# A transformer block on one core: W_out streamed over three and four raw places with low halves on VectorE alone, and the first sums of the second MLP product in other PSUM banks

## The chip, the cores and the metric

The kernel runs on one core of a Trainium2 chip. Its time is the device time of one execution in microseconds (us); 1531.92 us is the median of three runs. A profile is one execution recorded by the hardware profiler: PE is TensorE's matmuls, PEld its weight loads, DVE is VectorE, ACT is ScalarE, POOL is GpSimd, SP is the engine that issues most transfers.

## The reference

One block over x of 1024 tokens and 1024 features, all in float32:

```
u = rms_norm(x) * norm_mix_pre;   projections of u @ w_in
o_a = gated sparse attention;     o_b = sliding-window attention with sinks
y = sigmoid(gate_a) * (o_a @ w_up_nsa) + sigmoid(gate_b) * (o_b @ w_up_swa)
h = x + rms_norm(y @ w_out) * norm_mix_post
u = rms_norm(h) * norm_mlp_pre
f = square(relu(u @ w_mlp_in)) @ w_mlp_out
out = h + rms_norm(f) * norm_mlp_post
```

The change touches y @ w_out, and the first sums of the product with w_mlp_out.

## The kernel before, in words

Products run at nearly full float32 precision: each operand is split into a high half (a copy rounded to the matmul's input type, `wh`) and a low half (the operand less its high half, `wl`), and a product is three matmuls, high by high, high by low and low by high (`mm3`, lines 123 to 126). `split` (line 84) makes both halves: ScalarE copies, VectorE or GpSimd subtracts. `load_w` (line 96) loads a stretch of a weight into a tile called `wraw`, from a pool and with a number of places that the caller gives, and splits it. With no engine named it lets ScalarE make the high half (line 108) and deals out the subtraction (lines 115 and 116): five eighths to VectorE and three eighths to GpSimd. With an engine named it calls `split`, whose instructions have lines 87 and 91.

After attention the kernel computes y, transposed, in two halves of 512 tokens (`yh`, `yl`), line 773 on. At dc = 5 it already loads the first two rows of blocks of W_out into the pool `wo` (`wo_load`, two places) and splits the first.

`out_proj(c, ts_, nhs, xs_, at)`, line 837, is one pass of y @ W_out: two blocks of 128 tokens by all 1024 features, in four PSUM banks. It runs over eight steps k2. A step is one row of blocks of W_out, [128, 1024], 512 KB: a transfer, a split, and 12 matmuls (two token blocks, two halves of the features, three each). Four passes follow one another, c = 0 with blocks 0, 1 and then 2, 3, and c = 1 likewise, and each streams W_out anew. In pass 1 (`started` is empty) steps 0 and 1 use what `wo` holds, and steps 2 to 7 load into two places of the pool `wp2`, their halves into two places of `wp2`. From pass 2 on all eight steps load into the same two raw places, and the halves go into three places (`WEB`) of the pool `we`, which is opened after pass 1, when `wo` is closed. The low halves of c = 0 are dealt out to VectorE and GpSimd, those of c = 1 go to VectorE.

At the end of a pass ScalarE takes the sum of squares of each bank (line 874) and VectorE multiplies the bank by the gain (line 875). Then, for each block, come `norm_a` (residual h and its sum of squares, lines 884 to 894, with a store of h issued by GpSimd), `norm_b` (the second norm, line 899) and `norm_t` (eight transposes on TensorE, line 909, in two PSUM banks of their own with the tag `pt`, and splits of them). `load_x` loads rows of x; at step `at` of passes 1 and 2 ScalarE's queue issues it, held behind the last high half by `tc.issue_after(last_act[0].ins)` (line 851). `rstd_of` (line 139) has small instructions on both engines.

Behind the passes stand four `head`s of the MLP's first product (line 1004), then a loop over 16 blocks `mlp1` (line 1059), which makes a product of 2 x 2 blocks with seven products instead of eight, from sums and differences of its operands (`factor`, line 923, and lines 1065 and 1092). Their sums stand in PSUM tiles with the tag `ps`, six banks used in turn. The second product (`product`, line 1205) also has seven parts; the first, fifth, sixth and seventh add up in four banks `xs`, the others in four banks `ys`. Before, `xs` is allocated first, then `ys`.

The instructions of each engine stand in one order, fixed when the program is built: a list scheduler walks through the program with an estimate of how long things take, and gives each engine the first of its instructions, in program order, that is ready by that estimate. On the chip each engine then goes through its own list and waits where it must. Tiles with the same tag share places; a new one waits until the last reader of the old one is done.

Of the kernel before, what the change touches and what calls it, by code (L numbers as in the profile page):

```python
# [8 lines left out]
F32 = mybir.dt.float32  # L9
F32R = mybir.dt.float32r  # L10
AF = mybir.ActivationFunctionType
ALU = mybir.AluOpType
# [3 lines left out]
P = 128  # L16
T = 1024
D = 1024
NB = T // P
# [9 lines left out]
CUT = (5, 5)  # L29
# [5 lines left out]
WEB = 3  # L35
# [17 lines left out]
def tile_hybrid_block(ctx: ExitStack, tc: tile.TileContext, x, norm_mix_pre, norm_mix_post, norm_mlp_pre,  # L53
                      norm_mlp_post, w_in, cmp_pos_k, cmp_w1_k, cmp_w2_k, cmp_pos_v, cmp_w1_v, cmp_w2_v,
                      attn_sinks, rel_bias, w_up_nsa, w_up_swa, w_out, w_mlp_in, w_mlp_out, onehot, out):
    nc = tc.nc
# [3 lines left out]
    def pool(name, bufs=1, side="left", space=None):  # L60
        kw = {} if space is None else {"space": space}
        if space is not DRAM:
            kw["reuse_waits"] = "tile"
        if space is None:
            kw["side"] = side
        return tc.tile_pool(name=name, bufs=bufs, **kw)
# [17 lines left out]
    def split(h, l, src, h_eng="act", l_eng="dve"):  # L84

        if h_eng == "act":
            nc.scalar.activation(h, src, AF.Copy)  # L87
        else:
            nc.vector.tensor_copy(h, src)
        eng = nc.vector if l_eng == "dve" else nc.gpsimd  # L90
        eng.tensor_tensor(l, src, h.bitcast(F32), op=ALU.subtract)  # L91

    nw = [0]
    last_act = [None]

    def load_w(parts, shape, wpool=None, hb=2, l_eng=None, rpool=None, rb=2, cut=5, tag="w"):

        raw = (rpool or wp).tile([P] + shape, F32, name="wraw", tag="wraw", bufs=rb)
        for sl, ap in parts:
            nc.sync.dma_start(raw[sl] if sl is not None else raw, ap)  # L100
        wpool = wpool or wp
        h = wpool.tile([P] + shape, F32R, name="wh", tag=tag + "h", bufs=hb)
        l = wpool.tile([P] + shape, F32R, name="wl", tag=tag + "l", bufs=hb)
        nw[0] += 1
        if l_eng:
            split(h, l, raw, l_eng=l_eng)
        else:
            last_act[0] = nc.scalar.activation(h, raw, AF.Copy)
            if len(shape) == 1:
                hv, lv, rv = (t.rearrange("p (a b) -> p a b", a=8) for t in (h, l, raw))  # L110
            elif shape[0] < 8:
                hv, lv, rv = (t.rearrange("p k (a b) -> p (k a) b", a=8 // shape[0]) for t in (h, l, raw))
            else:
                hv, lv, rv = h, l, raw
            for eng, a, b in ((nc.vector, 0, cut), (nc.gpsimd, cut, 8)):
                eng.tensor_tensor(lv[:, a:b], rv[:, a:b], hv[:, a:b].bitcast(F32), op=ALU.subtract)
        return h, l
# [5 lines left out]
    def mm3(ps, ah, al, bh, bl, first, last):  # L123
        nc.tensor.matmul(ps, ah, bh, start=first, stop=False)  # L124
        nc.tensor.matmul(ps, ah, bl, start=False, stop=False)  # L125
        nc.tensor.matmul(ps, al, bh, start=False, stop=last)  # L126
# [27 lines left out]
    def transpose_split(ps_pool, tag, u, th, tl, b0, bufs):  # L154

        for k0 in range(0, NB, 4):
            pt = ps_pool.tile([P, 4, P], F32, name="pt", tag=tag, bufs=bufs)
            for j in range(4):
                nc.tensor.transpose(pt[:, j, :], u[:, (k0 + j) * P:(k0 + j + 1) * P], ident)
            split(th[:, k0:k0 + 4, b0:b0 + P], tl[:, k0:k0 + 4, b0:b0 + P], pt)  # L160
# [9 lines left out]
    with ExitStack() as s_u:  # L170
# [36 lines left out]
        with ExitStack() as s:  # L207
# [16 lines left out]
            def v_weights():  # L224
                for k in range(0, NB, 2):
                    raw = wp.tile([P, 2, NV], F32, name="vraw", tag="wraw", bufs=2)
                    for a, b, c in ((0, 128, C_VS), (128, 280, C_VW), (280, 408, C_VB)):
                        nc.sync.dma_start(raw[:, :, a:b], wr[:, k:k + 2, c:c + b - a])
                    split(vh[:, k:k + 2, :], vl[:, k:k + 2, :], raw)
# [180 lines left out]
        with ExitStack() as s:  # L410
# [328 lines left out]
            op = s_ot.enter_context(pool("ot"))  # L739
# [12 lines left out]
    with ExitStack() as s:  # L752
# [6 lines left out]
        wo = s_wo.enter_context(pool("wo", side="right"))  # L759
# [11 lines left out]
        with s_ot:  # L771
            dp = s_ot.enter_context(pool("dtmp"))
            for dc in range(8):
# [11 lines left out]
                for c in range(2):  # L785
                    ts = slice(c * 512, (c + 1) * 512)
                    t = []
# [26 lines left out]
        wp2 = s_w2.enter_context(pool("wq"))  # L814
# [12 lines left out]
        ep = s_e.enter_context(pool("etmp"))  # L827
# [1 line left out]
        eh = s_e.enter_context(pool("etmph"))  # L829
        hb_e.update({b: eh.tile([P, D], F32, name="hb", tag="hb", bufs=2) for b in (0, 1)})  # L830
        s_we = s_e.enter_context(ExitStack())
        ssp = [ep.tile([P, 2], F32, name="ssp", tag="ssp", bufs=8) for _ in range(NB)]

        hbs = {}
        started, we = [], []

        def out_proj(c, ts_, nhs, xs_=(), at=0):
            pss = {(t, nh): ps_any() for t in ts_ for nh in nhs}
            n = 1024 // (512 * len(nhs))
            for k2 in range(NB // n):  # L840
                if started or k2 > 1:
                    wh, wl = load_w([(None, wor[:, n * k2:n * k2 + n, 512 * nhs[0]:512 * nhs[-1] + 512])],
                                    [n, 512 * len(nhs)], *((we[0], WEB) if started else (wp2, 2)), cut=CUT[c],
                                    rpool=wp2, l_eng="dve" if c else None)
                elif k2:
                    wh, wl = (wp2.tile([P, 1, 1024], F32R, name=n_, tag="w" + n_[1], bufs=2) for n_ in ("wh", "wl"))
                    split(wh, wl, wo_raw[1])
                else:
                    wh, wl = wo_hl
                if k2 == at:  # L850
                    with tc.issue_after(last_act[0].ins):
                        for b in xs_:
                            load_x(b, nc.scalar)
                for j in range(n):
                    k = n * k2 + j
                    for t in ts_:
                        ts = slice(t * P, (t + 1) * P)
                        for i, nh in enumerate(nhs):
                            ns = slice(i * 512, (i + 1) * 512)
                            mm3(pss[t, nh], yh[c][:, k, ts], yl[c][:, k, ts], wh[:, j, ns], wl[:, j, ns],  # L860
                                k == 0, k == NB - 1)
            if not started:
                s_wo.close()
                we.append(s_we.enter_context(pool("we")))
            started.append(1)
            for t in ts_:
                b = c * 4 + t
                if b not in o1:
                    o1[b] = (ea if b % 4 < 2 else ep).tile([P, D], F32, name="o1",
                                                           tag="o1a" if b % 4 < 2 else "o1b", bufs=2)  # L870
                for nh in nhs:
                    ns = slice(nh * 512, (nh + 1) * 512)
                    junk = we[0].tile([P, 512], F32, name="junk", tag="junk", bufs=1)
                    nc.scalar.activation(junk, pss[t, nh], AF.Square, accum_out=ssp[b][:, nh:nh + 1])
                    nc.vector.tensor_tensor(o1[b][:, ns], pss[t, nh], gpost[:, ns], op=ALU.mult)
# [4 lines left out]
        def load_x(b, eng=None):  # L880
            hbs[b] = hb_e[b] if b in hb_e else (eh if b < 4 else ea).tile([P, D], F32, name="hb", tag="hb", bufs=2)
            (eng or nc.sync).dma_start(hbs[b], x[b * P:(b + 1) * P, :])
# [40 lines left out]
        def factor(i, b):  # L923
# [17 lines left out]
            split(bh[i][:, :, hs], bl[i][:, :, hs], src)  # L941

        out_proj(0, (0, 1), (0, 1), (0, 1), 4)
        norm_a(0)
        norm_a(1)
        norm_b(0)
        norm_b(1)
        load_x(2)
        load_x(3)
        out_proj(0, (2, 3), (0, 1), (4, 5), 3)  # L950
        norm_t(0)
        norm_t(1)
        norm_a(2)
        norm_a(3)
        norm_b(2)
        norm_b(3)
        out_proj(1, (0, 1), (0, 1))
        norm_t(2)
        norm_t(3)
# [193 lines left out]
            return p.tile([P, 2, 512], F32R, name=name, tag=name, bufs=n)  # L1153

        pq = s.enter_context(pool("ps3", space=PSUM))
        xs = [pq.tile([P, 512], F32, name=f"xs{t}") for t in range(4)]
        ys = [pq.tile([P, 512], F32, name=f"ys{t}") for t in range(4)]
        w2v = w_mlp_out.rearrange("(q e p) (j c) -> e j p q c", e=2, p=P, j=2)
        NK = NPAIR // 2
        b2 = {}  # L1160
# [170 lines left out]
```

## Time and profile before

| what | value |
|---|---|
| median of three runs | 1531.92 us (1530.36 to 1532.13) |
| the profiled execution, its own time | 1533.06 us |
| its span (first to last instruction) | 1531.3 us |
| mean granted TensorE clock | 0.989 of full |
| TensorE busy | 1472.2 us (96%) |
| VectorE, ScalarE, GpSimd busy | 1042.8, 792.9, 343.1 us |
| the four passes of y @ W_out | about 763.6 to 874.1 us of the span |
| the second product begins | 1215.35 us |

How to read it: a line of the profile names the line of the kernel, the engine, the operation, the tile written and the tiles read. A line can be that of a helper. "Idle before <- X" is the time for which the engine had nothing to do and the instruction that ended it. The chain is followed back from the last instruction, at each step to what released it.

### The profile page before, as it was taken

Reading aid. Unit: us, or ns where it says so; the run is one execution under the profiler, and the core shown is the slowest. Engines: PE = TensorE matmul, PEld = TensorE weight load, DVE = VectorE, ACT = ScalarE, POOL = GpSimd, SP = SyncE. Lnnn points to the kernel's source line nnn. Section 1 sums busy time; section 2 is a strip of 40 time slices with the busy share of each in tenths; the row PEclk is TensorE's granted clock in tenths of the full one; section 3 lists DMA queues with packets and bytes.
Section 4 is the critical chain, followed back from the end, with each engine's and each line's share of the span. In section 5 each row is a group of like instructions: output and inputs, shape, how many; then the busy total and the mean of one; then the engine's idle time right before and its main releaser. Section 6 shows DMA issues by size and latency. Waiting matters only on the chain.

```text
span 1531.3 us, 19921 instructions
## 1 busy us (share of the span) xinstructions
PE 1472.2 (96%) x6924; PEld 1205.1 (79%) x6924; DVE 1042.8 (68%) x2094; ACT 792.9 (52%) x1529; POOL 343.1 (22%) x281
## 2 busy tenths in 40 slices
PE   8998999999999999999989968999999999999997
PEld 6997888778887788888866756888888788888886
DVE  7454774588855988737547789866666655594775
ACT  5343775598854988664346663333322334334533
POOL 2000451100001000031042015775655300000302
PEclk9999999999999999999999988999999999999999
DMA  8723125111132111174256662453443696353551
GB/s 241 236 88 83 39 53 158 42 39 38 39 97 58 44 35 42 32 271 165 82 201 240 209 175 83 159 176 126 162 150 122 235 376 241 110 192 98 172 172 55
DMA packets 161335, 204.27 MB, mean 133 GB/s; under 512 B 14801, under 2 KB 104945, under 8 KB 161234
## 3 DMA queue, kind: packets, MB, share of 16 engines
q1 hardware_dynamic: 152880, 178.05, 36.8%
q0 software_dynamic: 7344, 21.53, 4.1%
q10 hardware_dynamic: 1010, 3.41, 0.6%
q8 instruction: 54, 0.88, 0.2%
q14 instruction: 47, 0.39, 0.1%
HBM read 152.50 MB, written 58.32 MB: 138 GB/s over the span
## 4 chain that ended last, share of the span: by engine, by line
PE 81%; DVE 7%; DMA 6%; ACT 3%; issue 2%; POOL 1%; SPq 0%; DVEq 0%; ACTq 0%; POOLq 0%
PE xs L1224 10%; PE ys L1224 9%; PE mm L124 7%; PE mm L125 7%; PE mm L126 7%; PE ps L1000 6%; PE ps L998 6%; PE ps L999 6%; PE pt L532 5%; DMA wraw<-in_w_out_dram 4%; PE o L545 2%; PE o L544 2%; PE s L499 2%; PE s L500 2%; PE ps L126 2%
## 5 line engine op out<-in xcount | busy, mean ns | idle before, releaser
L124 PE MATMUL mm<-uh,wh 128*128 128x512 f32 x464 | 200.0, 431 | 4.1 <-DVE qb L458 3.2
L126 PE MATMUL mm<-uh,wl 128*128 128x512 f32 x464 | 183.9, 397 | 0.0
L125 PE MATMUL mm<-ul,wh 128*128 128x512 f32 x464 | 183.7, 396 | 0.0
L91 DVE TENSOR_TENSOR tl<-pt,th 128x512 fp32r<-128x512 f32 x162 | 110.5, 686 | 42.3 <-ACT th L87 41.4
L512 ACT ACTIVATE e<-e,nm 128x256 f32<-128x256 f32 (+7 forms) x192 | 124.2, 649 | 19.9 <-DVE nm L506 19.5
L87 ACT ACTIVATE wh<-wraw 128x1024 fp32r<-128x1024 f32 x71 | 75.2, 1058 | 109.4 <-PE mm L125 36.7
L91 POOL TENSOR_TENSOR wl<-wraw,wh 128x1024 fp32r<-128x1024 f32 x16 | 38.4, 2402 | 413.0 <-ACT wh L87 381.1
L87 ACT ACTIVATE th<-pt 128x512 fp32r<-128x512 f32 (+1 forms) x178 | 104.2, 591 | 51.0 <-PE pt L532 43.3
L87 ACT ACTIVATE fh<-fraw 128x1024 fp32r<-128x1024 f32 x56 | 59.5, 1062 | 135.9 <-PE xs L1224 70.0
L91 DVE TENSOR_TENSOR fl<-fraw,fh 128x1024 fp32r<-128x1024 f32 x56 | 69.5, 1242 | 74.8 <-ACT fh L87 74.4
L126 PEld LDWEIGHTS mm<-uh,wl 128*128 128x128 f32 x464 | 87.4, 188 | 20.5
L1224 PE MATMUL xs<-vh,fh 128*128 128x512 f32 x256 | 100.3, 392 | 2.3 <-ACT c L1109 2.3
L91 DVE TENSOR_TENSOR wl<-wraw,wh 128x1024 fp32r<-128x1024 f32 x55 | 69.3, 1260 | 47.9 <-ACT wh L87 47.6
L532 PE MATMUL pt<-ident,e 128*128 128x128 f32 x648 | 101.1, 272 | 0.3 <-DVE tl L91 0.2
L124 PEld LDWEIGHTS mm<-uh,wh 128*128 128x128 f32 x464 | 88.0, 190 | 16.8 <-issue 3.3
L1224 PE MATMUL xs<-vl,fh 128*128 128x512 f32 x256 | 100.3, 392 | 0.0
L1224 PE MATMUL xs<-vh,fl 128*128 128x512 f32 x256 | 100.1, 391 | 0.0
L125 PEld LDWEIGHTS mm<-ul,wh 128*128 128x128 f32 x464 | 88.3, 190 | 11.8
L532 PEld LDWEIGHTS pt<-ident,e 128*128 128x128 f32 x648 | 80.7, 140 | 18.4 <-issue 0.5
L87 ACT ACTIVATE ws_h<-wraw 128x512 fp32r<-128x512 f32 x48 | 30.3, 631 | 118.8 <-PE ps L999 117.9
L1247 POOL TENSOR_TENSOR cc<-cc,gB 128x512 f32<-128x512 f32 x14 | 24.4, 1765 | 269.0 <-ACT sq L1246 267.3
L998 PE MATMUL ps<-bh,ws_h 128*128 128x512 f32 x192 | 77.7, 406 | 5.3 <-ACT ws_h L87 4.2
(298 smaller groups left out, 4011.4 us busy)
## 6 DMA issues: line engine op xcount, KB each, us to landing
fraw<-f_d SPq DMA_DIRECT2D x48, 512.0 KB, 3.6
wraw<-in_w_mlp_in_dram SPq DMA_DIRECT2D x36, 512.0 KB, 4.6
wraw<-in_w_out_dram SPq DMA_DIRECT2D x32, 512.0 KB, 3.5
f_d<-q SPq DMA_DIRECT2D x64, 256.0 KB, 3.8
b<-in_w_mlp_out_dram SPq DMA_DIRECT2D x32, 512.0 KB, 10.8
wraw<-in_w_in_dram SPq DMA_DIRECT2D x27, 512.0 KB, 4.7
f_d<-c SPq DMA_DIRECT2D x44, 256.0 KB, 4.3
gate_d<-gst SPq DMA_DIRECT2D x32, 256.0 KB, 2.0
```

The source lines that it names most:

```text
L87: nc.scalar.activation(h, src, AF.Copy)
L91: eng.tensor_tensor(l, src, h.bitcast(F32), op=ALU.subtract)
L124: nc.tensor.matmul(ps, ah, bh, start=first, stop=False)
L125: nc.tensor.matmul(ps, ah, bl, start=False, stop=False)
L126: nc.tensor.matmul(ps, al, bh, start=False, stop=last)
L499: nc.tensor.matmul(ps[:, :w], qs[r][:, qcol], kh, start=True, stop=False)
L512: nc.scalar.activation(e[:, :n], e[:, :n], AF.Exp, scale=-1.0, bias=nm[:, r:r + 1], accum_out=sm[:, r:r + 1])
L532: tr = nc.tensor.transpose(pt[:rows, r, :], es[r][:, off:off + rows], ident)
L998: nc.tensor.matmul(ps, ah[:, k, :], bh[i][:, k, :], start=n[0], stop=False, skip_group_check=True)
L999: nc.tensor.matmul(ps, ah[:, k, :], bl[i][:, k, :], start=False, stop=False, skip_group_check=True)
L1000: nc.tensor.matmul(ps, al[:, k, :], bh[i][:, k, :], start=False, stop=n[1], skip_group_check=True)
L1224: nc.tensor.matmul(bank[t], l_[:, j, ts], r_[:, j, :], start=a_, stop=z_, skip_group_check=True)
```

## The change

`out_proj` gets its raw places from other pools: steps 4 and 5 of pass 1 from `wo` (beside two of `wp2` for steps 2, 3, 6 and 7), and steps 2 and 5 of the later passes from a new place in `we` (beside two of `wp2`). All low halves of W_out go to VectorE, as `split` makes them, and `split` notes its high half in `last_act`. The sums of squares of eight blocks stand in two tiles instead of eight. In the second product `ys` is allocated first, and `xs` behind it, with its tiles 2 and 3 ahead of 0 and 1.

```diff
     def split(h, l, src, h_eng="act", l_eng="dve"):
         if h_eng == "act":
-            nc.scalar.activation(h, src, AF.Copy)
+            last_act[0] = nc.scalar.activation(h, src, AF.Copy)
...
-        eng.tensor_tensor(l, src, h.bitcast(F32), op=ALU.subtract)
+        return eng.tensor_tensor(l, src, h.bitcast(F32), op=ALU.subtract)
...
-        ssp = [ep.tile([P, 2], F32, name="ssp", tag="ssp", bufs=8) for _ in range(NB)]
+        ssps = [ep.tile([P, 4, 2], F32, name="ssp", tag="ssp", bufs=2) for _ in range(2)]
+        ssp = [ssps[b // 4][:, b % 4] for b in range(NB)]
...
                     wh, wl = load_w([(None, wor[:, n * k2:n * k2 + n, 512 * nhs[0]:512 * nhs[-1] + 512])],
-                                    [n, 512 * len(nhs)], *((we[0], WEB) if started else (wp2, 2)), cut=CUT[c],
-                                    rpool=wp2, l_eng="dve" if c else None)
+                                    [n, 512 * len(nhs)], *((we[0], WEB) if started else (wp2, 2)), l_eng="dve",
+                                    **(dict(rpool=we[0], rb=1) if started and k2 % 3 == 2 else
+                                       dict(rpool=wo) if not started and k2 % 4 < 2 else dict(rpool=wp2)))
...
-        xs = [pq.tile([P, 512], F32, name=f"xs{t}") for t in range(4)]
         ys = [pq.tile([P, 512], F32, name=f"ys{t}") for t in range(4)]
+        xs = [pq.tile([P, 512], F32, name=f"xs{t}") for t in (2, 3, 0, 1)]
+        xs = xs[2:] + xs[:2]
```

## Rows read from the trace of the kernel before

**Rows 1.** The profile's page: busy time of the engines; chain of waits by line.

```profile
PE 1472.2 (96%) x6924; PEld 1205.1 (79%) x6924; DVE 1042.8 (68%) x2094; ACT 792.9 (52%) x1529; POOL 343.1 (22%) x281
...
PE xs L1224 10%; PE ys L1224 9%; PE mm L124 7%; PE mm L125 7%; PE mm L126 7%; PE ps L1000 6%; PE ps L998 6%; PE ps L999 6%; PE pt L532 5%; DMA wraw<-in_w_out_dram 4%; PE o L545 2%; PE o L544 2%; PE s L499 2%; PE s L500 2%; PE ps L126 2%
```

**Rows 2.** The chain of waits, by line, from 760 to 880 us.

```profile
by line: DMA wraw<-in_w_out_dram 48.0%; POOL wl L116 9.7%; DVE wl L91 8.2%; ACT wh L87 7.9%; issue 6.8%; ACT wh L108 5.3%; DMA wraw<-in_w_mlp_in_dram 3.7%; ACT junk L874 2.3%; PE ps L1000 1.6%; PE ps L999 1.1%; PE ps L998 1.1%; ACT L143 1.1
```

**Rows 3.** Passes 1 to 4: us, busy PE to POOL, clock, DMA share, GB/s.

```profile
763.60:790.60 27.00, 23.41 (x98) 17.58 (x96) 8.35 (x10) 8.54 (x9) 9.83 (x6) 1.00 0.60 204
790.60:821.80 31.20, 26.80 (x112) 19.10 (x112) 21.38 (x38) 19.45 (x35) 14.80 (x10) 1.00 0.65 229
821.80:847.60 25.80, 24.96 (x113) 19.42 (x113) 22.12 (x39) 18.04 (x34) 1.11 (x2) 1.00 0.66 221
847.60:874.10 26.50, 23.95 (x106) 18.67 (x104) 18.50 (x35) 13.77 (x25) 1.06 (x2) 1.00 0.70 230
```

**Rows 4.** Timeline of TensorE, W_out stage: start, length, what, count, [idle before].

```profile
770.74 1.20 PE L124 MATMUL ps<-wh,yh 128*128 128x512 f32 x4 [1.34 <-ACT wh L108]
...
805.82 1.09 PE L909 MATMUL pt<-ident,o 128*128 128x128 f32 x8 [1.16 <-DVE rs_t L145]
...
834.27 1.10 PE L124 MATMUL ps<-wh,yh 128*128 128x512 f32 x4
...
837.09 1.03 PE L909 MATMUL pt<-ident,o 128*128 128x128 f32 x8
837.88 1.18 PE L124 MATMUL ps<-wh,yh 128*128 128x512 f32 x4
...
864.45 1.20 PE L124 MATMUL ps<-wh,yh 128*128 128x512 f32 x4 [2.46 <-ACT wh L87]
```

**Rows 5.** Tile wraw, 750 to 880 us: durations min/median/max in ns.

```profile
L87 ACT ACTIVATE wh<-wraw x19: 1051/1060/1066, 763.2 to 875.8; 128x1024 fp32r<-128x1024 f32 x19
L91 DVE TENSOR_TENSOR wl<-wraw,wh x19: 1216/1225/1227, 765.2 to 877.2; 128x1024 fp32r<-128x1024 f32 x19
...
L116 DVE TENSOR_TENSOR wl<-wraw,wh x14: 811/825/1645, 770.7 to 818.7; 128x640 fp32r<-128x640 f32 x14
L116 POOL TENSOR_TENSOR wl<-wraw,wh x14: 1600/1657/1967, 770.8 to 818.8; 128x384 fp32r<-128x384 f32 x14
...
DMA to landing us min/median/max: 3.4/3.6/8.9
```

**Rows 6.** TensorE's and VectorE's timelines around 1212 us; two stretches.

```profile
1209.99 0.50 PE L998 MATMUL ps<-bh7h,ws_h 128*128 128x512 f32 x1 [0.84 <-DVE c L1099]
...
1212.66 0.39 PE L1000 MATMUL ps<-bh7h,ws_l 128*128 128x512 f32 x1
1215.35 0.74 PE L1224 MATMUL xs<-vh,fh 128*128 128x512 f32 x1 [2.30 <-ACT c L1109]
...
1218.87 0.39 PE L1224 MATMUL xs<-vh,fl 128*128 128x512 f32 x1
...
1211.71 1.22 DVE L91 TENSOR_TENSOR vl<-b,vh 128x1024 fp32r<-128x1024 f32 x1
...
1215.40:1218.40 3.00, 3.00 (x7) 2.37 (x8) 3.00 (x5) 1.06 (x1) 0.72 (x1) 0.51 0.64 193
1219.00:1230.00 11.00, 11.00 (x50) 9.07 (x49) 8.32 (x10) 3.08 (x3) 3.60 (x5) 1.00 0.88 267
```

**Rows 7.** Entry of the block loop: TensorE's timeline, and one piece of the chain.

```profile
891.87 1.03 PE L909 MATMUL pt<-ident,o 128*128 128x128 f32 x8
...
893.15 10.31 DMA wraw<-in_w_mlp_in_dram
...
908.60 0.80 PE L998 MATMUL ps<-bh,s_h 128*128 128x512 f32 x1 [9.34 <-ACT p L1070]
```

**Rows 8.** One stretch of pass 2, columns as in rows 3.

```profile
800.00:810.00 10.00, 7.78 (x36) 5.63 (x35) 8.12 (x17) 5.34 (x10) 4.48 (x4) 1.00 0.83 313
```

**Rows 9.** Timeline of VectorE in pass 3: the first block's L899.

```profile
835.43 1.28 DVE L899 SCALAR_TENSOR_TENSOR o<-hb,rs_o,gpre 128x1024 f32<-128x1024 f32 x1
```

## The prediction

> **What bounds the kernel now.** I read the page first [rows 1]. TensorE is busy for 1472.2 of 1531.3 us, so only some 59 us can be won by giving it work sooner; everything else must come from a slow clock or from fewer instructions, and the change removes none of its matmuls. The chain by line puts 4% on transfers of W_out, and that is the one place where a transfer ends the waits. So I read the chain for 760 to 880 us alone, the stage of y @ W_out [rows 2]: 48% of it is the landing of W_out, 9.7% GpSimd's low halves, 13% ScalarE's high halves. The chain goes around: raw place filled, high half, low half, raw place free, next transfer.
>
> Then the stretches, one for each of the four passes of out_proj [rows 3]. TensorE idles 3.6, 4.4, 0.8 and 2.6 us in them (length less busy). But busy counts pipelined matmuls whole, so I take the pure length from the timeline [rows 4]: one step of W_out's rows (12 matmuls) goes from 834.27 to 837.09, so 2.82 us, and eight make 22.6 us; a block's eight transposes take 0.79 us (837.09 to 837.88). The four passes took 27.0, 31.2, 25.8 and 26.5 us, together 110.5; pure they are 4 x 22.6 and the 40 transposes in them 4.0, so 94.4. **16.1 us is slack**, and it is the most that the first part can give.
>
> Why two raw places don't do: a transfer lands in 3.6 us (median), the high half takes 1.06, GpSimd's three eighths 1.66 beside VectorE's five eighths of 0.83 [rows 5]. One place turns around in 6.3 us, so two give a step each 3.2 us, where TensorE wants one each 2.82.
>
> The other place is the change to the second product [rows 6]. Its first matmul comes at 1215.35 after 2.30 us of idleness ended by ScalarE's L1109, which reads the last sums out of the bank that xs0 gets. Its operands were there: the last of them, vl, which only the second matmul reads, ended at 1212.93. Then eight matmuls come 0.44 us apart, with a granted clock of 0.51 (the level of 1.2 GHz) from 1215.4 to 1218.4 and 1.00 (2.4 GHz) behind it: 1218.87 less 1215.35 is 3.52 us, where eight matmuls take 8/12 of a step's 2.82, that is 1.88.
>
> **The change, part by part.**
>
> Pass 1 (steps 2 to 7 over four places, 4 and 5 in the two that steps 0 and 1 leave). Step 2 can't come sooner: it waits for the same memory, and its wait of 1.34 us stays [rows 4]. The rest of the slack goes: 22.6 + 1.4 is 24.0, a gain of 3.0. The low half in VectorE takes 1.22 instead of 0.83 and 1.66 [rows 5]; with 8.4 of 27 us busy there [rows 3] this has cover.
>
> Pass 2 (three places, low halves on VectorE alone). It then does just what pass 3 does before: the same eight splits in VectorE, two blocks of norms, 16 transposes. Pass 3 took 25.8 with two places, so I take 25.8 instead of 31.2: a gain of 5.4. VectorE's busy time there is 21.4 of 31.2 [rows 3], of which GpSimd beside it is part: a low half of 825 ns took up to 1645 [rows 5]. Eight longer subtractions add 8 x 0.40 = 3.2 us.
>
> Pass 3: VectorE is busy 22.1 of 25.8 us, so I count no gain. Pass 4: its one long wait, 2.46 us at 864.45 for a high half whose transfer was late [rows 4], goes with a third place: 2.4. Sum of the passes: 3.0 + 5.4 + 0 + 2.4 = **10.8 us**. Bounds: all slack but the first wait, 14.7; at the other end the price of the 14 longer subtractions wholly on the path, 14 x 0.40 = 5.6, which leaves 5.2. The trace has no three-place pass. I take 10.8 since pass 3 is the nearest thing to it.
>
> Does it reach the end? After pass 4 come the norms of its two blocks, transposes, the heads' products, and a wait of 9.34 us of TensorE for the first sums of the block loop [rows 7]. The transfer ahead of that wait is issued at 893.15, after the transposes at 891.87, whose norms follow pass 4's end. All of that is tied to pass 4's end, not to a clock, so I count the gain through.
>
> Queues. SP issues the same transfers of W_out in this stage, only earlier; the two broadcasts of the gains stay ahead of step 2's. GpSimd loses 14 subtractions and keeps its stores of h, which wait for VectorE as before. `split` now notes its high half so that the loads of x on ScalarE's queue keep their place behind the same instruction: nothing. The sums of squares in two tiles instead of eight: nothing; if VectorE's read of one held up ScalarE's write of the next, it would cost ScalarE the length of that short read, and ScalarE is busy only 19.5 of 31.2 us in its fullest pass [rows 3].
>
> Second product. xs0 and xs1 move to the two banks of the norms' transposes, which no block of the loop uses, xs2 and xs3 to the two that the last block leaves alone, ys to the four others, whose first use is a product later. The wait of 2.30 us goes and with it, as I expect, the slow clock: 2.30 + 1.64 = **3.9 us**. Bounds: 2.3 if the clock falls anyway; 4.7 if the scheduler also fills the 0.84 us ahead of the last block's own last product [rows 6]. Late next is vl at 1212.93, just when TensorE is free (1212.66 + 0.39).
>
> **Sum:** 1533.06 (the profiled execution, 1531.3 of it span) - 10.8 - 3.9 = 1518.4 us. The median of the runs, 1531.92, lies 1.1 lower.
>
> **A rule that speaks against it.** In the stretch from 800 to 810 us the transfers moved 313 GB/s, a 512 KB load each 1.7 us [rows 8], and in the passes they move 204 to 230 GB/s at a share of 0.60 to 0.70 [rows 3]. So loads in flight together do add up, and 2.82 us a step is within reach.
> The Trainium skill says otherwise on SBUF — State Buffer, section "Can I just issue two DMAs to hit both halves?": all transfers land on the same 16 engines, and two at once serialize. By it more places would only move the wait; the first trace row speaks against it as far as 1.7 us a load, and what it would give is the first rival.
>
> **The rivals.**
> 1. *Transfers serialize at the pace of pass 3* (25.8 / 8 = 3.2 us a load). Pass 1 gains 27.0 - 25.8 = 1.2, pass 2 5.4, pass 4 0.7: 7.3 and 3.9, so 1521.9. For it: one of these loads took 8.9 us to land [rows 5], when several were under way. Against: 313 GB/s.
> 2. *VectorE is the bound.* The 5.6 us of longer subtractions lie on the path: 5.2 + 3.9, so 1524.0. For it: 22.1 of 25.8 us in pass 3. Against: pass 1 has room.
> 3. *Given back at the block loop.* If the loads behind 893.15 or VectorE's backlog decide there, the 9.34 us wait [rows 7] grows by what the passes gave: 1533.06 - 3.9 = 1529.2, no change that can be measured. Against: that issue hangs on the transposes.
> 4. *Slower: transposes too early in TensorE's queue.* The scheduler writes TensorE's order from its own estimate. A block's transposes need its norm chain, which after pass 2's end (821.8) came to the end of L899 at 836.7 [rows 9], 14.9 us on. At 805.82 TensorE already waited 1.16 for it [rows 4]. If loads no longer make holes in the estimate and the transposes land after three steps (8.5 us), they wait 6.4 us in each of four places (passes 2 to 4, the heads): 25.6 - 14.7, so 1544.0. It decides from 3.7 us a place (14.7 over four), that is placed before 11.2 us into a pass. Against: matmuls that are ready go first by program order.
> 5. *The banks aren't those*, and the second product waits as before: 1522.3.
>
> **Chances.** Forecast 0.58 (1512 to 1521); rivals 1 to 5: 0.08, 0.12, 0.10, 0.07, 0.05. About 0.2% (3.1 us) is what a measurement of this kernel can tell from no change. The forecast and rivals 1, 2 and 5 are faster, 0.83; rival 3, at 1529.2, is within 0.2% of 1531.92, 0.10; rival 4 is slower, 0.07. The range goes from 1512 (all slack but the first wait, and 4.7, would be 1513.7; the first wait too, 1512.3) to 1527, past rivals 1, 2 and 5; rivals 3 and 4 stay outside.
>
> **What would show it.** Right: the four passes at about 24, 26, 26 and 24 us; no GpSimd subtraction between 760 and 820; SP's raw issues two or three ahead of the split; the block loop's wait still near 9 us; xs's first matmul within 0.3 us of the last of ps and without the slow clock. Wrong: TensorE waiting before transposes for VectorE's norms by more than 3 us in several passes; pass 2 still near 31 with VectorE full; a longer wait ahead of the block loop; xs still ended by L1109. The forecast falls as a whole if the W_out stage ends less than 5 us earlier.

## The result, and the profile after

The changed kernel takes 1517.16 us (median of 4 runs, 1516.63 to 1520.16) beside 1532.03 us of the kernel before (4 runs, 1530.36 to 1533.84): a ratio of 0.9913, 95% interval 0.99 to 0.9925. The forecast was 1518.4, its range 1512 to 1527. The total is right to 1.2 us, but two of its terms are not, and with a third that was left out they nearly cancel.

The profiled executions are 15.7 us apart in span (1531.3 and 1515.6). Cut at five points, both traces tell where:

| stretch | before, us | after, us | gain |
|---|---|---|---|
| start to the first matmul of y @ W_out | 763.69 | 764.12 | -0.4 |
| that to the heads' first matmul (four passes) | 110.47 | 95.79 | 14.7 |
| that to the block loop's last matmul | 338.50 | 336.43 | 2.1 |
| that to part 5 of the second product, the third to run | 91.46 | 92.15 | -0.7 |
| that to the end | 227.18 | 227.11 | 0.1 |

The parts of the second product are called by their numbers in the program; they run in the order 1, 2, 5, 3, 6, 4, 7.

One execution stands for its kernel only to 2 or 3 us. The four passes took 93.9 to 96.5 us in the nine traces of this document whose W_out code is the changed one, and 110.5 and 108.6 in the two with the old code (the kernel before and experiment 2). The third stretch took 335.9 to 337.9 in the nine, 338.5 and 338.1 in the two.

**The four passes.** The page of the changed kernel, first its busy times; against [rows 1] GpSimd has 14 instructions fewer, TensorE as many as before.

```profile
PE 1469.0 (97%) x6924; PEld 1206.6 (80%) x6924; DVE 1048.0 (69%) x2094; ACT 791.5 (52%) x1529; POOL 321.7 (21%) x267
```

The windows of its passes 1 to 4, columns as in [rows 3]:

```profile
764.10:788.10 24.00, 22.86 (x97) 17.88 (x96) 11.76 (x12) 9.78 (x12) 0.00 (x0) 1.00 0.68 237
788.10:812.10 24.00, 24.00 (x112) 19.52 (x111) 20.01 (x37) 17.57 (x30) 1.17 (x2) 1.00 0.85 307
812.10:835.50 23.40, 23.40 (x108) 19.03 (x106) 20.94 (x39) 16.43 (x30) 1.06 (x2) 1.00 0.66 226
835.50:859.90 24.40, 24.33 (x113) 19.46 (x111) 18.98 (x37) 15.39 (x29) 1.06 (x2) 1.00 0.73 236
```

The second number is the length, the third TensorE's busy time. In passes 2 and 3 they are equal, where [rows 3] had 4.4 and 0.8 us between them. VectorE is nearly as busy as before (20.0 and 20.9 us, 21.4 and 22.1 in [rows 3]) in a shorter pass, and TensorE doesn't wait for it. Some transposes have moved from pass 3 to pass 4 (108 and 113 instructions of TensorE, 113 and 106 before), so about 0.5 us of pass 3's gain is only that. The matmul and transpose rows of TensorE's timeline that answer to [rows 4] are these; the first carries the one wait that is left in the stage, 1.08 us. Behind it, transposes enter 17.8 and 23.3 us into pass 2 without a wait:

```profile
770.91 1.20 PE L124 MATMUL ps<-wh,yh 128*128 128x512 f32 x4 [1.08 <-ACT wh L87]
...
805.86 1.03 PE L911 MATMUL pt<-ident,o 128*128 128x128 f32 x8
...
811.39 1.03 PE L911 MATMUL pt<-ident,o 128*128 128x128 f32 x8
```

The chain by line for 760 to 880 us, against [rows 2]: matmuls now lead, and the landing of W_out has fallen from 48.0 to 11.2%.

```profile
by line: PE ps L125 17.7%; PE ps L126 17.7%; PE ps L124 16.7%; DMA wraw<-in_w_out_dram 11.2%; PE ps L1002 5.2%; DVE wl L91 5.1%; PE ps L1000 4.6%; PE ps L1001 4.6%; DMA wraw<-in_w_mlp_in_dram 4.5%; PE pt L911 3.6%; ACT wh L87 3.5%; issue 1.
```

Tile wraw, 750 to 866 us: all 33 low halves are VectorE's, 1.22 us each, and a load lands in 4.7 us where it took 3.6 [rows 5]. Each load is slower, and the stage is faster, since more of them are under way.

```profile
L91 DVE TENSOR_TENSOR wl<-wraw,wh x33: 1206/1224/1227, 765.6 to 861.6; 128x1024 fp32r<-128x1024 f32 x33
...
DMA to landing us min/median/max: 3.3/4.7/7.8
```

**The second product.** TensorE's timeline around 1196 us: the first matmul into xs follows the block loop's last (1196.34) after 0.23 us; the wait for ScalarE of [rows 6] and its slow clock are gone. But 52.3 us behind that last matmul, in part 2 (ys), a new one stands, for the high half of f:

```profile
1193.66 0.50 PE L1000 MATMUL ps<-bh7h,ws_h 128*128 128x512 f32 x1 [0.84 <-DVE c L1101]
...
1196.57 0.39 PE L1228 MATMUL xs<-vh,fh 128*128 128x512 f32 x1
...
1248.66 0.50 PE L1228 MATMUL ys<-vh,fh 128*128 128x512 f32 x1 [2.95 <-ACT fh L87]
```

The chain from 1205 to 1252 us tells what it hung on (start, length, what): two loads of b, then one of f, each of the last two 10.8 us long.

```profile
1210.66 15.20 DMA b<-in_w_mlp_out_dram
...
1225.88 10.82 DMA b<-in_w_mlp_out_dram
...
1236.77 10.76 DMA fraw<-f_d
...
1247.55 1.07 ACT fh L87
```

Windows of the same kernel: from 1216 the transfers are full, 387 GB/s, and behind the wait the clock is at 0.62.

```profile
1216.00:1226.00 10.00, 10.00 (x46) 8.29 (x45) 4.37 (x4) 5.29 (x6) 0.00 (x0) 1.00 1.04 388
...
1236.00:1250.00 14.00, 11.05 (x48) 8.81 (x47) 13.24 (x13) 5.51 (x8) 0.00 (x0) 0.98 1.05 387
1250.00:1290.00 40.00, 40.00 (x172) 32.94 (x171) 21.90 (x21) 16.68 (x17) 0.00 (x0) 0.96 0.62 214
...
1248.70:1252.00 3.30, 3.30 (x10) 2.58 (x11) 3.17 (x3) 2.96 (x3) 0.00 (x0) 0.62 1.05 387
```

SP's timeline (start, length, what, count) shows the order: part 2's first load of f goes out behind six loads of b, the others behind eleven more. Those eleven take SP 14.70 us, 1.3 us each, and its waits from 1185 to 1262 us are in good part for earlier loads of b to land (9.0 us in 13 waits).

```profile
1208.81 4.47 SPq L1169 DMA_DIRECT2D b<-in_w_mlp_out_dram  x6
1213.62 7.68 SPq L1200 DMA_DIRECT2D fraw<-f_d  x1
1221.34 14.70 SPq L1169 DMA_DIRECT2D b<-in_w_mlp_out_dram  x11
1236.77 3.09 SPq L1200 DMA_DIRECT2D fraw<-f_d  x3
```

In the kernel before, SP's timeline has the same order at the same distance from the block loop's last matmul (1253.11 less 1212.66 is 40.45; here 1236.77 less 1196.34 is 40.43):

```profile
1253.11 3.08 SPq L1196 DMA_DIRECT2D fraw<-f_d  x3
```

**The entry of the block loop**, against [rows 7]: the wait is 6.16 us instead of 9.34, and in the chain no transfer of W_mlp_in lies ahead of it any more.

```profile
891.18 0.79 PE L1000 MATMUL ps<-bh,s_h 128*128 128x512 f32 x1 [6.16 <-ACT p L1072]
```

### The profile page after: what moved, and what is told of

The parts are those of the page before. It is cut to its first block, busy times and chain, and to the rows that moved or that the text cites. A ratio compares the mean times of both kernels' runs of the same rounds, so it can differ in the third digit from the quotient of the medians.

```text
span 1515.6 us, 19885 instructions
## 1 busy us (share of the span) xinstructions
PE 1469.0 (97%) x6924; PEld 1206.6 (80%) x6924; DVE 1048.0 (69%) x2094; ACT 791.5 (52%) x1529; POOL 321.7 (21%) x267
## 4 chain that ended last, share of the span: by engine, by line
PE 83%; DVE 8%; DMA 5%; ACT 2%; issue 2%; SPq 0%; DVEq 0%; POOL 0%; ACTq 0%
PE ys L1228 8%; PE xs L1228 7%; PE mm L124 7%; PE mm L125 7%; PE mm L126 7%; PE ps L1002 6%; PE ps L1000 6%; PE ps L1001 6%; PE pt L532 5%; PE ps L125 3%; PE ps L126 3%; PE ps L124 3%; PE o L545 2%; PE o L544 2%; PE s L499 2%; PE s L500 2%
## 5 line engine op out<-in xcount | busy, mean ns | idle before, releaser
L87 ACT ACTIVATE wh<-wraw 128x1024 fp32r<-128x1024 f32 x85 | 89.7, 1058 | 116.9 <-PE mm L125 36.7
L91 DVE TENSOR_TENSOR tl<-pt,th 128x512 fp32r<-128x512 f32 x162 | 110.5, 687 | 42.2 <-ACT th L87 41.3
L87 ACT ACTIVATE th<-pt 128x512 fp32r<-128x512 f32 (+1 forms) x178 | 104.2, 592 | 51.0 <-PE pt L532 43.8
L91 DVE TENSOR_TENSOR wl<-wraw,wh 128x1024 fp32r<-128x1024 f32 x69 | 86.3, 1252 | 57.6 <-ACT wh L87 57.3
L91 DVE TENSOR_TENSOR vl<-b,vh 128x1024 fp32r<-128x1024 f32 x56 | 69.2, 1238 | 19.9 <-ACT vh L87 19.9
## 6 DMA issues: line engine op xcount, KB each, us to landing
b<-in_w_mlp_out_dram SPq DMA_DIRECT2D x32, 512.0 KB, 10.8
```

Source lines behind the costliest of these rows:

```text
L87: last_act[0] = nc.scalar.activation(h, src, AF.Copy)
L91: return eng.tensor_tensor(l, src, h.bitcast(F32), op=ALU.subtract)
```

## The experiments

Each kernel was timed in several rounds beside the kernel before on the same chip. Three questions: what is each half of the change worth, what in the first half carries it, and what does the second half lack. The sums of squares in two tiles and the noting of `split`'s high half were not tried alone; experiment 4 has both, and all of the change but the places comes to 1.8 us there.

**1. The W_out half alone** (`e1_wout_only`: the changed kernel with the banks of before).

```diff
-        ys = [pq.tile([P, 512], F32, name=f"ys{t}") for t in range(4)]
-        xs = [pq.tile([P, 512], F32, name=f"xs{t}") for t in (2, 3, 0, 1)]
-        xs = xs[2:] + xs[:2]
+        xs = [pq.tile([P, 512], F32, name=f"xs{t}") for t in range(4)]
+        ys = [pq.tile([P, 512], F32, name=f"ys{t}") for t in range(4)]
```

> The W_out part alone: xs and ys stand in the banks of before. Theory (the banks' gain is given back in the second product, whose operands come at the pace of the transfers): the same as the whole change within 2 us, 1515 to 1519; the first matmul of xs waits about 2.3 us for L1109 again, and the 3.0 us wait of ys for fh is gone. Rival (the forecast on record, 3.9 us from the banks): about 1521, 3.9 us above the whole change.

Measured: 1517.14 us (5 runs, 1515.92 to 1517.63), ratio 0.9912 (0.9899 to 0.9926): as fast as the whole change. The old wait is back, and the new one gone.

```profile
1198.70 0.50 PE L1226 MATMUL xs<-vh,fh 128*128 128x512 f32 x1 [2.29 <-ACT c L1111]
```

**2. The banks alone** (`e2_banks_only`: the same lines, the other way, in the kernel before).

> The banks alone, with W_out streamed as before. Theory (given back): 1531 to 1533, no change from before within 1 us; xs's first matmul follows the last of ps at once and without the slow clock, and a new wait of 2.5 to 3.5 us of ys for fh stands in the second part of the second product, followed by eight matmuls at a granted clock near 0.5. Rival (the forecast): 1528, 3.9 us faster, with no new wait.

Measured: 1530.74 us (11 runs, 1527.47 to 1533.02), ratio 0.9994 (0.9983 to 1.0006): no gain that can be told from nothing, and the interval's end, 2.6 us, is below the 3.9 of the forecast. The wait for f stands here too, a little shorter than expected, so it comes with the banks and not with W_out:

```profile
1261.99 0.50 PE L1226 MATMUL ys<-vh,fh 128*128 128x512 f32 x1 [2.11 <-ACT fh L87]
```

**3. The new places, with low halves dealt as before** (`e3_places_dealt`: of the whole change, passes 1 and 2 give three eighths of each low half to GpSimd).

```diff
-  l_eng="dve",
+  l_eng="dve" if c else None, cut=CUT[c],
```

> The whole change, but the low halves of the first two passes are dealt out to VectorE and GpSimd again. Theory (raw places carry the gain of the W_out stage, the engine of the low halves does little): three places that turn around in some 6.5 us give a step each 2.2 us, under TensorE's 2.82, so the four passes take 95 to 99 us and the time is 1517 to 1521. Rival (taking the low halves from GpSimd, with its collisions with VectorE, carries pass 2): pass 2 stays at 27 to 31 us and the time is 1521 to 1525.

Measured: 1520.1 us (4 runs, 1515.32 to 1520.49), ratio 0.9925 (0.9908 to 0.9942); the stage takes 99.2 us, the passes 22.6, 26.2, 25.5 and 24.9. That is the theory's upper end, and pass 2 is shorter than the rival had it. The windows of passes 1 to 3:

```profile
764.10:786.70 22.60, 22.60 (x98) 17.95 (x97) 9.10 (x12) 9.19 (x11) 10.55 (x7) 1.00 0.72 243
786.70:812.90 26.20, 24.82 (x106) 18.22 (x104) 18.59 (x35) 14.49 (x24) 11.48 (x10) 1.00 0.78 263
812.90:838.40 25.50, 23.81 (x104) 18.78 (x105) 21.80 (x39) 17.99 (x33) 1.11 (x2) 1.00 0.70 236
```

The two passes that the edit touches take 48.8 us together (with five transposes fewer in them), where the whole change takes 48.0; the rest of the difference lies in passes 3 and 4, whose own code is the same.

**4. Two raw places, with low halves on VectorE** (`e4_two_places`).

```diff
-  **(dict(rpool=we[0], rb=1) if started and k2 % 3 == 2 else
-     dict(rpool=wo) if not started and k2 % 4 < 2 else dict(rpool=wp2)))
+  rpool=wp2)
```

> The whole change, but W_out keeps its two raw places in all passes; low halves on VectorE alone. Theory (raw places carry it): a place turns around in 3.6 + 1.06 + 1.22 = 5.9 us, two give a step each 2.95 us, so all passes look like passes 3 and 4 of before (25.8 and 26.5), together 103 to 106 us instead of 95.8, and the time is 1524 to 1528. Rival (the engine of the low halves carries it): the passes stay under 98 us and the time is 1517 to 1520.

Measured: 1527.76 us (10 runs, 1526.33 to 1533.92), ratio 0.9988 (0.9978 to 0.9999). The stage takes 108.6 us, longer than expected, and TensorE's wait late in pass 4, 2.93 us, answers to the 2.46 of [rows 4]. The windows of passes 2 and 3 (three of the stage's matmul records are missing, so a boundary may be 0.7 us off):

```profile
789.90:819.60 29.70, 26.30 (x114) 18.91 (x113) 21.17 (x39) 19.34 (x34) 1.18 (x2) 1.00 0.74 246
819.60:846.30 26.70, 25.59 (x112) 19.33 (x113) 21.73 (x39) 17.52 (x33) 1.06 (x2) 1.00 0.60 198
```

VectorE has as much to do in these two passes (21.2 and 21.7 us) as in the whole change (20.0 and 20.9); with a third place they take 24.0 and 23.4 us instead of 29.7 and 26.7. So the places decide: they carry 108.6 less 95.8, that is 12.8 of the 14.7 us. What the low halves on VectorE carry is not shown. The 1.9 us that are left are no more than the difference of two executions with the old code (experiment 2's stage, with dealt low halves, also took 108.6), and the 3.4 us of experiment 3 (99.2 less 95.8) lie for the most part in passes that its edit doesn't touch. All of the change but the places is 1.8 us by this run's ratio.

**5. Four places in pass 1, two in the others** (`e8_no_we_place`).

```diff
-  **(dict(rpool=we[0], rb=1) if started and k2 % 3 == 2 else
-     dict(rpool=wo) if not started and k2 % 4 < 2 else dict(rpool=wp2)))
+  rpool=wp2 if started or k2 % 4 > 1 else wo)
```

> The whole change without the third place of passes 2 to 4; pass 1 keeps its four. Theory (places carry it, each in its own pass): pass 1 takes about 24 us as in the whole change, passes 2 to 4 take 29, 27 and 27 as with two places in all passes, the stage 105 to 109, and the time is 1523 to 1527. Rival (what pass 1 gains lets the rest run ahead): the stage stays under 101 us and the time under 1521.

Measured: 1524.2 us (4 runs, 1521.95 to 1525.77), ratio 0.996 (0.9947 to 0.9972); the stage takes 103.2 us, the passes 23.1, 29.5, 25.6 and 25.0 (six records are missing, so a boundary may be 1.4 us off). The time is the theory's; the stage is 2 us shorter than it had it, in passes 3 and 4. The windows of passes 1 and 2:

```profile
763.80:786.90 23.10, 23.10 (x101) 18.64 (x100) 12.58 (x13) 10.35 (x14) 0.00 (x0) 1.00 0.63 221
786.90:816.40 29.50, 26.45 (x117) 19.69 (x116) 22.44 (x41) 20.09 (x36) 1.18 (x2) 1.00 0.74 255
```

The third place of passes 2 to 4 alone is worth 103.2 less 95.8, 7.4 us, most of it (5.5) in pass 2.

**6. Part 2's f on another queue.** If only its place in SP's line made f late, another queue would mend it: GpSimd's (`e5_fraw2_pool`), ScalarE's (`e6_fraw2_act`), and GpSimd's with the broadcast of the last gain written later in the program (`e7_fraw2_gb_late`).

```diff
-            eng = nc.gpsimd if i == 1 else nc.sync
+            eng = nc.gpsimd if i in (1, 2) else nc.sync
```

> The whole change, and the left operand of the second part of the second product (fraw) is loaded through GpSimd's queue instead of SP's, where it stands behind eleven loads of the right operand. Theory (the wait of ys for fh is a place in SP's queue, and those eleven loads aren't due yet): the 3.0 us wait and the slow clock behind it go, so 3.5 to 4.6 us less than the whole change, 1512 to 1514. Rival (the transfers are full from 1206 to 1250 us, so that the bytes themselves decide): the wait stays at 2 us or more, or moves to vh, and the time is within 1 us of 1517.

> As the run before, but through ScalarE's queue, whose high halves then stand behind the loads' waits. Theory (a place in SP's queue): 1512 to 1515, with ScalarE's issues costing it some 0.3 us each, off the path. Rival (bytes decide): within 1 us of 1517. If this and the run before differ by more than 2 us, the issuing engine's own waits matter too.

> As the run with GpSimd's queue, and the broadcast of the last gain (512 KB) is issued behind the second part instead of ahead of the first. Theory (a place in the queue): no change from that run within 1 us. Rival (bytes decide): 512 KB at some 385 GB/s is 1.4 us less of transfers in the full stretch, so 1 to 2 us faster than that run.

Measured: 1520.63 us (5 runs), ratio 0.9935 (0.9923 to 0.9947); 1525.48 (5 runs), ratio 0.9969 (0.9957 to 0.9981); and 1521.53 (6 runs), ratio 0.9944 (0.9932 to 0.9956). All three are slower than the whole change (ratio 0.9913; the first one's interval just touches its interval), so that theory fell; the rival, with its 1517 us, fell too. The waits of the first two (one row from each timeline of TensorE):

```profile
1253.80 0.79 PE L1228 MATMUL ys<-vh,fl 128*128 128x512 f32 x1 [4.80 <-DVE fl L91]
```

```profile
1236.43 0.80 PE L1228 MATMUL xs<-vh,fh 128*128 128x512 f32 x1 [8.82 <-ACT vh L87]
```

In the first, f's low half (1252.53) stands in VectorE's order behind eight subtractions of b for a later part, and the chain hangs them on a load of b that lands at 1242.29. In the second, ScalarE issues a load of f at 1234.85, which the chain hangs on a load of b that lands at 1234.77, and only behind that issue makes the high half that TensorE waits for. The third moved nothing: the trace has the broadcast at the same place in SP's order (1208.52), so it tells nothing of those bytes.

**7. The loads that nobody needs yet, behind f** (`e9_b_behind_fraw2`). Nine of the 17 loads of b that SP issues ahead of all but the first load of part 2's f are for parts 3 and 5. 9 x 512 KB at 387 GB/s are 12.2 us of full transfers. Here SP issues them behind part 2's last load of f.

```diff
             if i == 3:
-                return load_b(1, 1, kc)
+                with tc.issue_after(last_f[2].ins):
+                    return load_b(1, 1, kc)
             if i == 5:
-                load_b(0, 1, kc)
+                with tc.issue_after(last_f[2].ins):
+                    load_b(0, 1, kc)
...
-            eng.dma_start(raw, f_d[i - 1][2 * kc:2 * kc + 2].rearrange("q p t -> p q t"))
+            last_f[i] = eng.dma_start(raw, f_d[i - 1][2 * kc:2 * kc + 2].rearrange("q p t -> p q t"))
```

> The whole change, and the operands of the second product that its parts 3 and 5 need (9 loads of b, 512 KB each, which SP issues before the second part's f) are issued behind the second part's f. Theory (part 2's f lands late because loads that nobody needs yet lie ahead of it while the transfers are full): the wait of 3.0 us ahead of the second part and the slow clock behind it go, 1512 to 1515 us. Rival (the transfers are full either way and all of these bytes are wanted soon): part 2 starts on time but a later part waits as long, 1516 to 1519. Third case (holding the loads back makes part 3 or 5 late by more than 3 us): above 1519.

Measured: 1513.19 us (5 runs, 1511.66 to 1517.29), ratio 0.9892 (0.9875 to 0.9909). TensorE doesn't wait in parts 1 and 2. SP's timeline and the windows of this kernel:

```profile
1222.70 2.51 SPq L1169 DMA_DIRECT2D b<-in_w_mlp_out_dram  x2
1226.11 23.53 SPq L1204 DMA_DIRECT2D fraw<-f_d  x7
1249.68 5.77 SPq L1169 DMA_DIRECT2D b<-in_w_mlp_out_dram  x9
```

```profile
1236.00:1250.00 14.00, 14.00 (x64) 11.58 (x63) 8.13 (x8) 8.98 (x11) 0.00 (x0) 1.00 0.48 154
1250.00:1290.00 40.00, 40.00 (x178) 33.13 (x177) 28.22 (x27) 14.23 (x14) 0.00 (x0) 1.00 0.90 318
```

The same bytes move later, from a stretch at 387 GB/s to one that had stood at 214, and TensorE is busy in all of both.

**8. The same with the banks of before** (`e10_b_behind_old_banks`: the edits of 1 and 7 together), to see what the banks are worth once the transfers have room.

> As the run e9_b_behind_fraw2, but with the banks of the second product as before the change. Theory (the banks are worth 2.3 to 3.9 us as soon as the transfers have room): this kernel is 2.3 to 3.9 us behind e9_b_behind_fraw2, with the wait of 2.3 us for L1111 ahead of xs. Rival (the transfers set the start of the later parts whatever the first does): the two within 1 us of each other.

Measured: 1517.37 us (5 runs, 1513.3 to 1518.7), ratio 0.9908 (0.9892 to 0.9923), 4.2 behind experiment 7 on the same chip. Only part of that is the banks': from the block loop's last matmul to part 5 its trace (of the slowest of its five executions) has 89.87 us, and experiment 7's has 87.28. That is 2.6 us, the old wait of 2.30 and little else. The other 2.1 us of the two profiled executions' difference lie ahead of that matmul, where the kernels have the same instructions.

```profile
1202.59 0.50 PE L1230 MATMUL xs<-vh,fh 128*128 128x512 f32 x1 [2.30 <-ACT c L1111]
```

**9. The change and experiment 7 once more, side by side** (`e11_change_again`, `e12_b_behind_again`), with no edit to either.

> The whole change once more, unaltered, on the same chip as e12_b_behind_again. Theory (its second product loses 3 us and a slow clock to loads that lie ahead of the second part's f): 1516 to 1518 us, 3 to 4.5 us behind e12_b_behind_again. Rival (the difference seen between the change and e9_b_behind_fraw2 is that of two chips): within 1 us of each other.

> The kernel of e9_b_behind_fraw2 once more, on the same chip as e11_change_again. Theory: 1512 to 1514 us, no wait of TensorE at the start of the second part. Rival: within 1 us of e11_change_again.

Measured: 1516.64 us (6 runs, 1512.83 to 1520.52) and 1513.55 us (5 runs, 1512.75 to 1514.95); ratios 0.9905 (0.9889 to 0.992) and 0.9884 (0.987 to 0.9899). The medians are 3.1 us apart, the low end of what the theory expected; the two ratios' intervals overlap a little. The profiled execution of `e11_change_again` was the quickest of its six; in it the wait for f is 2.04 us and no slow clock follows:

```profile
1245.67 0.50 PE L1228 MATMUL ys<-vh,fh 128*128 128x512 f32 x1 [2.04 <-ACT fh L87]
```

The second product in all kernels that leave the queues as they were, from the block loop's last matmul to the first of part 5, that is parts 1 and 2 (one part without a wait takes 43.52 us, two 87.0), and the granted clock in the 3 to 7 us from the end of the wait:

| kernel | us | TensorE's wait in it | clock behind it |
|---|---|---|---|
| before | 91.46 | 2.30 for c (xs) | 0.51 |
| whole change | 92.15 | 2.95 for fh (ys) | 0.62 |
| the same again | 89.66 | 2.04 for fh (ys) | 1.00 |
| W_out half alone | 91.44 | 2.29 for c (xs) | 0.58 |
| banks alone | 91.32 | 2.11 for fh (ys) | 0.66 |
| whole change, low halves dealt (3) | 91.91 | 2.72 for fh (ys) | 0.73 |
| whole change, two places (4) | 89.40 | 1.79 for fh (ys) | 1.00 |
| whole change, four places in pass 1 alone (5) | 89.32 | 1.73 for fh (ys) | 1.00 |
| b behind f | 87.28 | none | |
| the same again | 87.29 | none | |
| b behind f, old banks | 89.87 | 2.30 for c (xs) | 1.00 |

With the slow clock this takes 91.3 to 92.2 us, without it 89.3 to 89.9, whichever the banks. So at the same clock and the old order of the loads the banks are worth less than 1 us either way (the one trace with the old banks and no slow clock is experiment 8's), and a difference of some 2 us between two of these traces is the clock's, not theirs.

From there to the end every one of them takes 227.1 to 227.2 us, so what is won here stays won.

## Why the prediction was right, and where it was wrong

**Direction, range and place** were right: the raw places were the limit of the stage, and the gain reached the end. Of the forecast's signs, two came true (no GpSimd subtraction in pass 1, xs within 0.3 us of the last matmul of the loop); two didn't (passes 2 and 3 at about 26 us, the block loop's wait near 9).

**The passes: the term was 10.8 us, 14.7 were measured**, its upper bound to the tenth, which is luck as far as two executions can differ by 2 us. The passes came out at 24.0, 24.0, 23.4 and 24.4 where the text had 24.0, 25.8, 25.8 and 24.1. What failed is the step "Pass 2 then does just what pass 3 does before", with "VectorE is busy 22.1 of 25.8 us, so I count no gain" behind it. Pass 3 was taken as the pattern of a pass with VectorE near full, but it was itself a pass of two places. Experiment 4 shows it: the same VectorE work with two places takes 26.7 us there, with three 23.4. The prediction's own pure lengths would have told that there was something to win: eight steps and 16 transposes are 22.6 + 1.6 = 24.2, so the 25.8 of pass 3 held 1.6 us of slack, and the forecast put the same slack into pass 2. And the trace of the kernel before has it: its chain from 821 to 848 us, pass 3, is the ring of W_out's places and little else.

```profile
by line: DMA wraw<-in_w_out_dram 55.7%; ACT wh L87 19.8%; DVE wl L91 18.2%; issue 2.7%; ACT junk L874 2.2%; ACT braw L912 1.7%; ACTq L87 0.3%; DVE rs_t L145 0.1%; DVE rs_r L147 0.1%
```

VectorE stands in it with hardly more than the low halves, however busy it is. The transfers of this chain begin at 823.13, 828.91, 834.80 and 842.00, so a place turns around in 6.3 us in the mean, and two places give a step each 3.1 us, 25.2 for eight. (The 6.3 us of the prediction are another sum: they count GpSimd's 1.66, which pass 3 doesn't have.)

**The banks: the term was 3.9 us, they brought nothing** (experiments 1 and 2). The step "The wait of 2.30 us goes and with it the slow clock" was right as it stands. What was wrong is "Late next is vl": that looked only at the first two matmuls. Part 2's second load of f is issued 40.4 us behind the block loop's last matmul in both kernels, since SP's line hangs on the last block's stores and not on the second product (the transfer of the last gain, which follows those stores, goes out 12.0 us behind that matmul in both). In the kernel before, part 2 starts 47.9 us behind that matmul, and with the new banks 43.8 behind it; it meets f 5.6 us later. Its first matmul in the two kernels:

```profile
1260.60 0.39 PE L1224 MATMUL ys<-vh,fh 128*128 128x512 f32 x1
```

```profile
1240.11 0.39 PE L1228 MATMUL ys<-vh,fh 128*128 128x512 f32 x1
```

The matmul that waits could go at 52.3 (1248.66) and not before; by the old start it would have come at about 47.9 + 5.6 = 53.5. So there were some 1.2 us of slack, of the 4.2 that the banks tried to take, and the other 3.0 are the new wait. (In the other five traces with these banks and this order the matmul could go at 51.1 to 52.1, a slack of 1.4 to 2.4.) Experiment 7 shows that the order of the loads is the cause, and 8 that the banks are worth 2.6 us with that order mended. The slow clock, which made up the rest of the 3.9, didn't follow the wait there; it can, at the same matmul (W_out half alone), and is then worth 1.6 us more by the table (91.44 less 89.87).

**The entry of the block loop: counted at nothing, it gave 2.1.** "All of that is tied to pass 4's end" is not quite so. SP's first transfers of W_mlp_in go out 5.5 us ahead of the heads' first matmul before (868.61) and 6.6 ahead after (853.32), since the raw places come free sooner, and the wait for them left the chain. No run isolates this, so the cause is argued and not shown. The size is as uncertain: from the heads' first matmul to the loop's first it takes 29.7 to 31.3 us with the changed W_out code (34.4 and 34.0 with the old), and to the loop's last 335.9 to 337.9 (338.5 and 338.1).

So the total was right to 1.2 us because 3.9 us too little in one place and 2.1 missed in another stood against 4.6 too much in the third (the 0.4 us ahead of the stage are of no part of the change). That they nearly cancel is luck.

**The rivals.** 1 (transfers serialize) and 2 (VectorE) fall with passes 2 and 3, where TensorE is busy throughout; 3 with the shorter wait at the loop; 4 with the transposes that enter without a wait (its 1544.0 had left out the 3.9 us of the banks); 5 with xs. Nobody had named the rival that came: the change to the banks gives its gain back one part later. The Trainium skill's rule (SBUF — State Buffer, "Can I just issue two DMAs to hit both halves?") that two transfers at once serialize is not what the W_out stage shows: 512 KB loads one after another, at the 3.3 us of the shortest landing, would move some 159 GB/s (an estimate), and pass 2 moved 307 GB/s with loads that each took longer. It agrees better with the second product, where at 387 GB/s a load of b and one of f each took 10.8 us; there another order helped (experiment 7) and other queues did not (experiment 6).

**Still open:** why pass 3 of experiment 3, whose own code is that of the change, takes 25.5 us and not 23.4; what the low halves on VectorE are worth; and the 2 to 3 us by which executions of the same stage differ (93.9 to 96.5 us).

## What to carry to other kernels

Where a place, a split and a transfer go around in a ring, another place costs no work, and the pass that serves as a pattern for the gain must not be in the same ring. Before a product is started sooner, follow the operands of its later parts back to what issues them, and measure their slack: a start that is 4 us earlier is worth the slack alone. And where transfers are full, loads that run ahead of need delay those that are needed; here it helped to issue them behind, and not to send the needed ones through another queue.

## What the runs showed of the hardware that was not expected

- The clock behind a wait of some 2 to 3 us falls in some executions and not in others, even of one kernel. After 2.30 us in the kernel before it was granted 0.51 [rows 6]; after 2.95 us in the changed one 0.62, and 1.00 after 2.04 us in the same kernel's second trace; after the 2.46 us in pass 4 of before it stayed at 1.00 [rows 3, 4]. The clearest pair are the W_out half alone and experiment 8: the same wait at the same matmul (2.29 and 2.30 us), and granted 0.58 and 1.00. The windows of the two, in this order:

```profile
1198.70:1201.70 3.00, 3.00 (x8) 2.36 (x9) 3.00 (x5) 1.06 (x1) 0.72 (x1) 0.58 0.70 195
```

```profile
1202.60:1205.60 3.00, 3.00 (x13) 2.51 (x14) 3.00 (x5) 1.06 (x1) 0.72 (x1) 1.00 0.66 186
```

Nor does the longer wait decide: one matmul of the block loop waits 2.63 us in the changed kernel (922.63) and 2.35 us in experiment 7 (922.66), and the clock falls behind the shorter wait. The windows behind it, the changed kernel first:

```profile
924.00:927.00 3.00, 3.00 (x15) 2.40 (x14) 3.00 (x6) 0.63 (x1) 0.00 (x0) 1.00 0.36 102
```

```profile
924.00:927.00 3.00, 3.00 (x10) 2.31 (x10) 3.00 (x6) 0.49 (x1) 0.00 (x0) 0.69 0.37 96
```

So the price of such a wait lies between its length and about 2 us more, and no row here tells which it will be.
- A load of 512 KB lands in 3.6 us with few others under way [rows 5], in 4.7 with three or four places in use, and in 10.8 with the transfers full at 387 GB/s.
